# Modulation vectors that are made in later stages, and GpSimd taking one of the two streams throughout

## The chip, the core and the metric

The kernel runs on one core of one Trainium2 chip. The metric is the device time of one execution in microseconds (us). The core has five engines with an instruction queue each: TensorE (PE: matmuls; PEld: its weight loads), VectorE (DVE), ScalarE (ACT), GpSimd (POOL) and SyncE (SP), which here issues all DMA transfers. Each queue is worked off in its written order; an instruction waits until what it needs has been signalled, and everything behind it on that queue waits with it.

## The reference

Two token streams, 256 context tokens and 256 latent tokens of width 1024, go through two layers. Each layer is a feed-forward sub-layer, a token mixer (four branches) and a second feed-forward sub-layer. Every sub-layer is modulated by vectors that a small product makes from a conditioning vector:

```python
act_l = jax.nn.silu(c)
act_c = jax.nn.silu(c_ctx)
for i in range(DEPTH):
    mod_l = (act_l @ w_mod[i] + b_mod[i])[:, None, :]              # nine vectors of 1024
    mod_c = (act_c @ w_mod[i][:, :n_c] + b_mod[i][:n_c])[None, None, :]
    ...
def ffn_sublayer(x, mods, base, g_pre, g_post, w_in, w_out):
    h = modulated_norm(x, g_pre, mods[base], mods[base + 1])       # shift, scale
    return x + 0.5 * mods[base + 2] * rms_norm(swiglu(h, w_in, w_out), g_post)   # gate
```

So a layer has nine modulation vectors for each stream: 0 to 2 (shift, scale, gate) for the first feed-forward sub-layer, 3 to 5 for the mixer, 6 to 8 for the second feed-forward sub-layer. In the last layer the context stream needs only 0 to 4. A vector of both streams takes one 1024 x 1024 block of `w_mod`, 4 MB.

## The kernel before

**Stages.** The program runs through feed-forward stage 1 (layer 0, first), mixer 0, feed-forward stage 2 (layer 0, second), feed-forward stage 3 (layer 1, first), mixer 1 and feed-forward stage 4. Below, "stage" means one of the feed-forward stages. All of them are the function `ffn`, for 512 tokens (the fourth for 256).

**A unit.** In `ffn` a loop runs over 22 slices `f` of the hidden width, called units here. A unit loads two weight tiles of 128 x 1024 (`fin`, 512 KB each), and each is split into a high part and a rest: `wchunk` has ScalarE copy `raw` to `wh` (L220) and VectorE subtract (`wl`, L222). Three matmuls (L228 to L230) for each of eight slices of the width and two weight tiles make the 48 matmuls of a unit. Then ScalarE takes a tanh of the result (L487), VectorE finishes the gated product (L488, L489) and splits it (`gg`). Behind the 22 units stands the output part (`outproj`, 16 weight tiles `foa` and six `fob`, then the norm that begins the next stage).

**The four slots.** Every weight tile and every tile of `w_mod` is loaded into the same rotating buffer, tag `raw`, with four slots (`rp = pool(st, "rp", 4)`). SP's queue issues the loads in order; a load waits there until the last user of its slot is done.

**The modulation vectors.** `mod_steps(l, js, act)` makes vectors `js` of layer `l` in steps. A step loads one 128 x 1024 tile of `w_mod`, eight steps a vector. For the latent stream (`s = 1`) VectorE multiplies the tile by the activation row and sums along it in one instruction (L274, output `jk`). For the context stream (`s = 0`) either GpSimd multiplies in place (L279) and ScalarE sums (L280), or, for layer 0 and `j >= JB = 5`, VectorE does a second product. Where only the latent stream is needed (layer 1, `j >= 5`), even steps go to VectorE and odd ones to GpSimd and ScalarE.

**Who calls the steps.** `stepper(gens, total, skip)` hands out the steps. After each unit `ffn` calls it with weight 2, in the output part with weight `OW = 1` after each of 16 chunks; the first `skip` calls do nothing, and the others add `steps / total` times the weight. The steps start in `st0` (stage 1), `st1` (stage 2) and `st2` (stage 3). PE's order is written out by hand; the other queues are ordered by a scheduler that may move a step ahead by some instructions.

**Who needs the vectors.** `gate_rows(l, base, ...)` in unit 19 of a stage reads vector `base + 2`; `fill0`, `fill1` and `fill2` behind the last unit build the shift and scale of what comes next (`pre_coeff`), used in the norm at the end of the output part. `act_load` loads the two activation rows into the two buffers of `xp`, tag `xr`, which the residual rows `xr` of a stage use too.

Of the kernel before, what the change touches and what calls it, by code (L numbers as in the profile page):

```python
# [79 lines left out]
RAW0 = 16  # L80
WPF = 2
OW = 1.0
JB = 5


def layout(i):
# [77 lines left out]
def build(tc, A):  # L164
# [10 lines left out]
    def dma(o, i):  # L175
        return nc.sync.dma_start(o, i)
# [8 lines left out]
    with st, tc.manual_schedule(engines={mybir.EngineType.PE}):  # L185
# [74 lines left out]
        def mod_steps(l, js, act, raw=None):  # L260
            if callable(act):
                act = act()
            for j in js:
                ss = [1] if l == 1 and j >= 5 else [0, 1]
                for k in range(KT):
                    w = raw() if raw else rp.tile([P, D], F32, tag="raw", name="raw")
                    dma(w, A["wmod"][l, j, k])
                    c = j * KT + k
                    both = l == 0 and j >= JB
                    for s in ss if both else [1]:  # L270
                        if 0 not in ss and k % 2:
                            continue
                        jk = sp.tile([P, D], BF16, tag="sq", name="jk", bufs=1)
                        V.scalar_tensor_tensor(  # L274
                            jk, w, 0.5, act[s], op0=ALU.mult, op1=ALU.mult, accum_out=md[l][:, s, c : c + 1]
                        )
                    if not both and (0 in ss or k % 2):
                        s = ss[0]
                        G.tensor_tensor(w, w, act[s], op=ALU.mult)  # L279
                        S.activation(w, w, AF.Copy, scale=0.5, accum_out=md[l][:, s, c : c + 1])  # L280
                    n = 4 if raw else KT
                    if (k + 1) % n == 0:
                        for s in ss:
                            m = md[l][:, s, c + 1 - n : c + 1]
                            V.tensor_tensor(m, m, bmt[l][:, c + 1 - n : c + 1], op=ALU.add)
                    yield

        def pre_coeff(l, base, gi, streams):
            a = cp.tile([P, 2, KT], F32, tag="pa", name="pa", bufs=2)
            for s in streams:  # L290
                V.scalar_tensor_tensor(
                    a[:, s], md[l][:, s, (base + 1) * KT : (base + 2) * KT], 1.0, ngt[l][:, gi], op0=ALU.add, op1=ALU.mult
                )
                V.tensor_scalar(a[:, s], a[:, s], RMS_D, None, op0=ALU.mult)
            return lambda s, k: (a[:, s, k : k + 1], md[l][:, s, base * KT + k : base * KT + k + 1])

        def gate_rows(l, base, gi, fac, streams):
            gr = cp.tile([P, 2, D], F32, tag="grow", name="grow", bufs=1)
            gc = cp.tile([P, 2, KT], F32, tag="gc", name="gc", bufs=2)
            for s in streams:  # L300
                V.scalar_tensor_tensor(
                    gc[:, s], md[l][:, s, (base + 2) * KT : (base + 3) * KT], fac * RMS_D, ngt[l][:, gi], op0=ALU.mult, op1=ALU.mult
                )
            s0, n = streams[0], len(streams)
            ps = psy.tile([P, 512], F32, tag="py", name="psg")
            T.transpose(ps[: n * KT, :P], gc[:, s0:].rearrange("p s k -> p (s k)"), ident)
            gs = sp.tile([P, 512], F32, tag="t", name="gs")[:, :P]
            S.activation(gs[: n * KT], ps[: n * KT, :P], AF.Copy)
            gd = dp.tile([1, 2 * D], F32, tag="gd", name="gd", bufs=2)
            dma(gd[:, : n * D].rearrange("o (k p) -> (o k) p", p=P), gs[: n * KT])  # L310
            dma(gr[:, s0:].rearrange("p s d -> p (s d)"), gd[:, : n * D].to_broadcast([P, n * D]))
            return gr

        def new_h():
            hh = hp.tile([P, KT, NTOK], F32R, tag="hh", name="hh")
            hl = hp.tile([P, KT, NTOK], F32R, tag="hl", name="hl")
            return hh, hl
# [220 lines left out]
        def act_load():  # L538
            a = [xp.tile([P, D], F32, tag="xr", name="act") for _ in range(2)]
            for s in range(2):  # L540
                dma(a[s], actd[s].to_broadcast([P, D]))
            return a
# [4 lines left out]
        def stepper(gens, total, skip=0):  # L547

            todo = [g for g, _ in gens]
            rate = sum(c for _, c in gens) / total  # L550
            state = {"credit": 0.0, "skip": skip}

            def step(weight):
                if state["skip"]:
                    state["skip"] -= 1
                    return
                state["credit"] += rate * weight
                while todo and state["credit"] > 1e-6:
                    try:
                        next(todo[0])  # L560
                        state["credit"] -= 1.0
                    except StopIteration:
                        todo.pop(0)

            return step
# [15 lines left out]
        with ExitStack() as fs:  # L581
            with ExitStack() as s0:
# [22 lines left out]
                for t in TALL:  # L605
                    xs0[t] = tp.tile([P, D], F32, name=f"x0_{t}")
                raw0 = lambda: tp.tile([P, D], F32, tag="raw0", name="raw0", bufs=RAW0)
                ms0 = mod_steps(0, [0], act, raw0)
                pm = [psy.tile([P, 512], F32, tag="py", name="pm1") for _ in range(2)]

# [95 lines left out]
            def acts0():  # L706
# [2 lines left out]
                        acts.extend(act_load())  # L709
                return acts  # L710

            st0 = stepper([(mod_steps(0, [2, 3, 4], acts0), 24), (mod_steps(0, [5, 6, 7, 8], acts0), 32)], 46, 6)

            def step0(w):
                st0(w)
# [7 lines left out]
        for l in range(L):  # L723
            last = l == L - 1
            toks = TLAT if last else TALL
            streams = [1] if last else [0, 1]

            nx = dict(src=xd, out=None, keep=toks)
            late = mixer(E, l, h, late, toks, streams, nx)
            h = nx["h"]  # L730

            with ExitStack() as fs:
                gp = Gates(fs, f"B{l}")
                if last:
                    n3 = dict(src=xd, out=A["out"], keep=[])
                    ffn(l, 1, h, late, toks, n3, gp, lambda w: None, lambda: gate_rows(l, 6, 5, 0.5, streams), lambda: None)
                else:
                    n3 = dict(src=xd, out=None, keep=TALL)

                    def fill1():  # L740
                        n3.update(coeff=pre_coeff(1, 0, 0, [0, 1]), h=new_h())

                    st1 = stepper([(mod_steps(1, [0, 1, 2, 3, 4], act_load), 40)], 50, 2)
                    late = ffn(l, 1, h, late, toks, n3, gp, st1, lambda: gate_rows(l, 6, 5, 0.5, streams), fill1)
                    h = n3["h"]
            if not last:
                with ExitStack() as fs:
                    gp = Gates(fs, "C")
                    n4 = dict(src=xd, out=None, keep=TLAT)

                    def fill2():
                        n4.update(coeff=pre_coeff(1, 3, 2, [0, 1]), h=new_h())

                    st2 = stepper([(mod_steps(1, [5, 6, 7, 8], act_load), 32)], 50, 2)
                    late = ffn(1, 0, h, late, TALL, n4, gp, st2, lambda: gate_rows(1, 0, 1, 0.5, [0, 1]), fill2)
                    h = n4["h"]

# [1212 lines left out]
```

## Time and profile before

| what | value |
|---|---|
| median of 3 runs | 2695.58 us (2693.67 to 2699.35) |
| the profiled execution | 2695.88 us, its span 2694.1 us |
| TensorE busy, share of the span | 2511.9 us, 93% |
| VectorE | 1765.9 us, 66% |
| ScalarE | 1097.6 us, 41% |
| GpSimd | 711.6 us, 26% |

The span runs from the first to the last instruction of the profiled execution; what the run's own time has beyond it lies before and after. Busy shares are averages over stages with different limits, so the stages are read apart. A busy TensorE is not one at its peak, because matmuls overlap and their ends are modelled: the pace of a stage is read from how long the same count of matmuls takes.

### The profile page before, as it was taken

The numbers are of one execution on the slowest core, as the hardware profiler recorded it, in microseconds if no ns is written. First come the engines' busy times: TensorE is split into PE (matmuls) and PEld (weight loads), VectorE is DVE, ScalarE is ACT, GpSimd is POOL, SyncE is SP. The second block draws the span as 40 slices with busy tenths as digits, with TensorE's granted clock in tenths as the row PEclk, the third lists the DMA queues.
The fourth block names the chain that finished last, engine by engine and source line by source line (L and its number), as shares of the span: only waits on it lengthen the run. The fifth ranks groups of instructions, "written<-read, shape, count | busy, mean of one in ns | idle before, by whom it ended". The sixth has DMA issues, their size and how long they took to land. (4 is left out here: it accounts for less than half of the span.)

```text
span 2694.1 us, 38024 instructions
## 1 busy us (share of the span) xinstructions
PE 2511.9 (93%) x14606; PEld 2113.7 (78%) x14606; DVE 1765.9 (66%) x2547; ACT 1097.6 (41%) x1868; POOL 711.6 (26%) x637
## 2 busy tenths in 40 slices
PE   6978999999999889999999999999999998778998
PEld 3856777887788667888777788888899897677997
DVE  6788885455646898457777555454355678986664
ACT  5435322454543233344343343333255553335443
POOL 4884100100102773002233301111010127860000
PEclk8989999999999999999999999999999998889999
DMA  6345666223232333344445545445423354335564
GB/s 235 106 152 187 212 219 210 83 79 79 79 110 71 85 99 101 94 160 145 164 147 174 179 157 160 160 156 184 137 73 100 108 176 134 114 110 182 162 189 148
DMA packets 134498, 378.55 MB, mean 141 GB/s; under 512 B 26679, under 2 KB 45864, under 8 KB 133548
## 3 DMA queue, kind: packets, MB, share of 16 engines
q1 hardware_dynamic: 134316, 376.11, 43.1%
q8 instruction: 115, 1.88, 0.3%
q14 instruction: 67, 0.55, 0.1%
HBM read 358.14 MB, written 17.91 MB: 140 GB/s over the span
## 5 line engine op out<-in xcount | busy, mean ns | idle before, releaser
L222 DVE TENSOR_TENSOR wl<-raw,wh 128x1024 fp32r<-128x1024 f32 x411 | 567.2, 1380 | 423.9 <-ACT wh L220 417.1
L220 ACT ACTIVATE wh<-raw 128x1024 fp32r<-128x1024 f32 x424 | 447.5, 1056 | 597.0 <-issue 166.0
L230 PE MATMUL pin<-hh,wl 128*128 128x512 f32 (+1 forms) x1468 | 531.5, 362 | 46.5 <-DVE wl L222 46.4
L228 PE MATMUL pin<-hh,wh 128*128 128x512 f32 (+1 forms) x1468 | 530.3, 361 | 8.9 <-DVE hh L356 6.8
L229 PE MATMUL pin<-hl,wh 128*128 128x512 f32 (+1 forms) x1468 | 529.0, 360 | 4.6 <-DVE hl L359 4.3
L279 POOL TENSOR_TENSOR raw<-raw,act 128x1024 f32<-128x1024 f32 x88 | 236.0, 2684 | 480.0 <-DVE jk L274 228.2
L230 PEld LDWEIGHTS pin<-hh,wl 128*128 128x128 f32 x1468 | 282.2, 192 | 96.1 <-DVE wl L222 56.5
L228 PEld LDWEIGHTS pin<-hh,wh 128*128 128x128 f32 x1468 | 282.5, 192 | 52.1 <-DVE hh L356 8.3
L229 PEld LDWEIGHTS pin<-hl,wh 128*128 128x128 f32 x1468 | 281.9, 192 | 47.3 <-DVE hl L359 7.0
L274 DVE SCALAR_TENSOR_TENSOR jk<-raw,act 128x1024 bf16<-128x1024 f32 x152 | 210.8, 1387 | 152.4 <-DMA raw<-wmod 143.2
L249 POOL TENSOR_TENSOR r<-v,mhalf 128x1 f32<-128x1 f32 (+2 forms) x46 | 31.6, 686 | 932.1 <-DVE v L248 833.4
L1090 PE MATMUL pm<-hh,wh 128*128 128x512 f32 (+1 forms) x704 | 254.9, 362 | 0.0
L1091 PE MATMUL pm<-hl,wh 128*128 128x512 f32 (+1 forms) x704 | 247.1, 351 | 0.0
L1092 PE MATMUL pm<-hh,wl 128*128 128x512 f32 (+1 forms) x704 | 246.8, 351 | 0.0
L280 ACT ACTIVATE raw<-raw 128x1024 f32<-128x1024 f32 x88 | 93.2, 1059 | 240.4 <-POOL raw L279 240.4
L403 PE MATMUL y<-wl,gg 128*128 128x512 f32 x448 | 178.2, 398 | 4.0 <-DVE wl L222 3.9
L402 PE MATMUL y<-wh,gg 128*128 128x512 f32 x448 | 177.3, 396 | 0.0
L404 PE MATMUL y<-wh,gg 128*128 128x512 f32 x448 | 177.1, 395 | 0.0
L1090 PEld LDWEIGHTS pm<-hh,wh 128*128 128x128 f32 x704 | 136.7, 194 | 18.3 <-issue 2.5
L1092 PEld LDWEIGHTS pm<-hh,wl 128*128 128x128 f32 x704 | 135.8, 193 | 17.5
L1091 PEld LDWEIGHTS pm<-hl,wh 128*128 128x128 f32 x704 | 136.3, 194 | 15.0
L403 PEld LDWEIGHTS y<-wl,gg 128*128 128x128 f32 x448 | 84.2, 188 | 27.7 <-DVE wl L222 7.9
(425 smaller groups left out, 4829.6 us busy)
## 6 DMA issues: line engine op xcount, KB each, us to landing
raw<-fin SPq DMA_DIRECT2D x176, 512.0 KB, 3.5
raw<-wmod SPq DMA_DIRECT2D x136, 512.0 KB, 4.2
raw<-winf SPq DMA_DIRECT2D x122, 512.0 KB, 3.6
raw<-foa SPq DMA_DIRECT2D x64, 512.0 KB, 3.8
raw<-wbr SPq DMA_DIRECT2D x32, 512.0 KB, 3.6
raw<-fob SPq DMA_DIRECT2D x24, 512.0 KB, 4.1
xd<-xr SPq DMA_DIRECT2D x16, 512.0 KB, 2.9
xr<-xd SPq DMA_DIRECT2D x16, 512.0 KB, 4.9
```

The source lines that it names most:

```text
L220: S.activation(wh, w, AF.Copy)
L222: (G if turns[1] and turns[0] % turns[1] == 0 else V).tensor_tensor(wl, w, wh.bitcast(F32), op=ALU.subtract)
L228: T.matmul(out, lhsT=lh, rhs=rh, start=first and i == 0, stop=False)
L229: T.matmul(out, lhsT=lh, rhs=rl, start=False, stop=False)
L230: T.matmul(out, lhsT=ll, rhs=rh, start=False, stop=last and i == n - 1)
L274: V.scalar_tensor_tensor(jk, w, 0.5, act[s], op0=ALU.mult, op1=ALU.mult, accum_out=md[l][:, s, c : c + 1])
L279: G.tensor_tensor(w, w, act[s], op=ALU.mult)
L402: T.matmul(o, lhsT=lh, rhs=rh, start=kt == 0, stop=False)
L403: T.matmul(o, lhsT=lh, rhs=rl, start=False, stop=False)
L1090: T.matmul(o, lhsT=lh, rhs=rh, start=i == 0, stop=False)
L1091: T.matmul(o, lhsT=lh, rhs=rl, start=False, stop=False)
L1092: T.matmul(o, lhsT=ll, rhs=rh, start=False, stop=i == n - 1)
```

## The change

Three things are edited. `JB` and the second VectorE product go, so that with two streams GpSimd and ScalarE always take the context stream. Vector 8 of layer 0 (8 steps) moves from stage 1 to stage 2. Vectors 2, 3 and 4 of layer 1 (24 steps) move from stage 2 to stage 3, ahead of the 32 steps that were there. The totals that set the rate change with it: 48 steps at 46, skip 6 (were 56); 24 steps at 40, skip 2 (were 40 at 50); 56 steps at 50, skip 2 (were 32). `acts1` and `acts2` load the activation rows once for both lists of a stage.

```diff
-JB = 5
...
                     c = j * KT + k
-                    both = l == 0 and j >= JB
-                    for s in ss if both else [1]:
-                        if 0 not in ss and k % 2:
-                            continue
+                    if 0 in ss or k % 2 == 0:
+                        s = 1
                         jk = sp.tile([P, D], BF16, tag="sq", name="jk", bufs=1)
                         V.scalar_tensor_tensor(
                             jk, w, 0.5, act[s], op0=ALU.mult, op1=ALU.mult, accum_out=md[l][:, s, c : c + 1]
                         )
-                    if not both and (0 in ss or k % 2):
+                    if 0 in ss or k % 2:
                         s = ss[0]
                         G.tensor_tensor(w, w, act[s], op=ALU.mult)
                         S.activation(w, w, AF.Copy, scale=0.5, accum_out=md[l][:, s, c : c + 1])
...
-            st0 = stepper([(mod_steps(0, [2, 3, 4], acts0), 24), (mod_steps(0, [5, 6, 7, 8], acts0), 32)], 46, 6)
+            st0 = stepper([(mod_steps(0, [2, 3, 4], acts0), 24), (mod_steps(0, [5, 6, 7], acts0), 24)], 46, 6)
...
+                    act1 = []
+
+                    def acts1():
+                        if not act1:
+                            act1.extend(act_load())
+                        return act1
...
-                    st1 = stepper([(mod_steps(1, [0, 1, 2, 3, 4], act_load), 40)], 50, 2)
+                    st1 = stepper([(mod_steps(0, [8], acts1), 8), (mod_steps(1, [0, 1], acts1), 16)], 40, 2)
...
-                    st2 = stepper([(mod_steps(1, [5, 6, 7, 8], act_load), 32)], 50, 2)
+                    st2 = stepper([(mod_steps(1, [2, 3, 4], acts2), 24), (mod_steps(1, [5, 6, 7, 8], acts2), 32)], 50, 2)
```

The instructions of TensorE stand in the same order as before. The places below are where the others moved. Lines of the changed kernel are up to three lower in number (L175 for L176, L221 for L222, L271 for L274).

SP's queue near the start of stage 2, before: `wmod` is a tile of a modulation step, `fin` a weight tile, the number is the buffer's name.

```order
L176 DMA raw_10821<-wmod 128x1024
L176 DMA raw_10827<-wmod 128x1024
L176 DMA raw_10833<-fin 128x1024
L176 DMA raw_10864<-fin 128x1024
L176 DMA raw_10902<-wmod 128x1024
L176 DMA raw_10908<-fin 128x1024
L176 DMA raw_10939<-fin 128x1024
```

The same place now:

```order
L175 DMA raw_10771<-wmod 128x1024
L175 DMA raw_10777<-fin 128x1024
L175 DMA raw_10808<-fin 128x1024
L175 DMA raw_10846<-wmod 128x1024
L175 DMA raw_10852<-fin 128x1024
L175 DMA raw_10883<-fin 128x1024
```

Units with two steps and with one took turns; now a unit has one step, and every fifth has two.

SP's queue near the start of stage 3, before:

```order
L176 DMA raw_13583<-wmod 128x1024
L176 DMA raw_13587<-fin 128x1024
L176 DMA raw_13618<-fin 128x1024
L176 DMA raw_13656<-wmod 128x1024
L176 DMA raw_13660<-fin 128x1024
L176 DMA raw_13691<-fin 128x1024
L176 DMA raw_13729<-wmod 128x1024
L176 DMA raw_13733<-wmod 128x1024
```

The same place now:

```order
L175 DMA raw_13605<-wmod 128x1024
L175 DMA raw_13613<-wmod 128x1024
L175 DMA raw_13619<-fin 128x1024
L175 DMA raw_13650<-fin 128x1024
L175 DMA raw_13688<-wmod 128x1024
L175 DMA raw_13694<-wmod 128x1024
L175 DMA raw_13700<-wmod 128x1024
L175 DMA raw_13706<-fin 128x1024
L175 DMA raw_13737<-fin 128x1024
```

Steps of one stream, one or two a unit, have become steps of two streams, two or three a unit, until the 24 of them are done; the steps of one stream follow at the same rate.

VectorE's queue in the output part of stage 1, before: `jk` is a product of a step (`act_1304` the context row, `act_1305` the latent row), `wl` the split of a weight tile.

```order
L274 SCALAR_TENSOR_TENSOR jk_2953,md0_95<-raw_2949,act_1305 128x1024
L222 TENSOR_TENSOR wl_2922<-raw_2919,wh_2921 128x1024
L274 SCALAR_TENSOR_TENSOR jk_2987,md0_95<-raw_2985,act_1304 128x1024
L274 SCALAR_TENSOR_TENSOR jk_2989,md0_95<-raw_2985,act_1305 128x1024
L274 SCALAR_TENSOR_TENSOR jk_2993,md0_95<-raw_2991,act_1304 128x1024
L222 TENSOR_TENSOR wl_2958<-raw_2955,wh_2957 128x1024
```

The same place now:

```order
L221 TENSOR_TENSOR wl_2920<-raw_2917,wh_2919 128x1024
L271 SCALAR_TENSOR_TENSOR jk_3023,md0_95<-raw_3021,act_1305 128x1024
L221 TENSOR_TENSOR wl_2956<-raw_2953,wh_2955 128x1024
L271 SCALAR_TENSOR_TENSOR jk_3059,md0_95<-raw_3057,act_1305 128x1024
L221 TENSOR_TENSOR wl_2994<-raw_2991,wh_2993 128x1024
```

Between two splits two to four products of VectorE have become one; the context products of these steps stand on GpSimd now.

## Rows read from the trace of the kernel before

**Rows 1.** Windows of stage 1 (three), stage 2 (two), stage 3 (two): start:end, length, busy

```profile
core 0: us, PE busy (x) PEld busy (x) DVE busy (x) ACT busy (x) POOL busy (x), PEclk, DMA share, GB/s
110.00:260.00 150.00, 122.89 (x494) 96.86 (x493) 120.64 (x161) 64.47 (x97) 108.05 (x96) 0.91 0.47 158
260.00:364.00 104.00, 95.69 (x414) 76.52 (x413) 90.41 (x138) 34.29 (x51) 13.86 (x4) 1.00 0.63 208
364.00:494.00 130.00, 125.91 (x546) 100.15 (x544) 86.45 (x138) 40.17 (x65) 3.45 (x7) 1.00 0.57 188
1216.40:1483.50 267.10, 250.78 (x1147) 206.60 (x1146) 199.56 (x208) 108.16 (x168) 85.30 (x36) 0.98 0.46 159
1483.50:1608.20 124.70, 124.69 (x545) 100.53 (x544) 62.37 (x82) 48.16 (x79) 25.32 (x13) 1.00 0.50 166
1608.00:1853.10 245.10, 243.09 (x1147) 203.98 (x1146) 128.75 (x162) 90.46 (x133) 38.64 (x16) 1.00 0.51 163
1853.10:1977.20 124.10, 124.10 (x545) 100.71 (x544) 50.36 (x68) 41.51 (x67) 8.11 (x8) 1.00 0.40 132
```

**Rows 2.** Matmuls of the projections: ns min/median/max, first and last start; stages 2, 3

```profile
L228 PE MATMUL pin<-hh,wh x376: 278/389/632, 1216.4 to 1482.7; 128*128 128x512 f32 x164, 128*128 128x256 f32 x24
...
L228 PE MATMUL pin<-hh,wh x376: 278/389/478, 1608.0 to 1852.3; 128*128 128x512 f32 x164, 128*128 128x256 f32 x24
```

**Rows 3.** Timeline of ScalarE, the tanh of a unit: start, length; stages 2, 3

```profile
1341.10 0.58 ACT L487 ACTIVATE t<-pin 128x512 f32<-128x512 f32 x1
...
1352.07 0.57 ACT L487 ACTIVATE t<-pin 128x512 f32<-128x512 f32 x1
...
1364.80 0.57 ACT L487 ACTIVATE t<-pin 128x512 f32<-128x512 f32 x1
...
1378.18 0.58 ACT L487 ACTIVATE t<-pin 128x512 f32<-128x512 f32 x1
...
1674.27 0.58 ACT L487 ACTIVATE t<-pin 128x512 f32<-128x512 f32 x1
...
1685.11 0.58 ACT L487 ACTIVATE t<-pin 128x512 f32<-128x512 f32 x1
```

**Rows 4.** Timeline of VectorE over one unit of stage 2 with two steps

```profile
1355.38 1.22 DVE L274 SCALAR_TENSOR_TENSOR jk<-raw,act 128x1024 bf16<-128x1024 f32 x1 [1.96 <-DMA raw<-wmod]
...
1357.13 3.10 DVE L274 SCALAR_TENSOR_TENSOR jk<-raw,act 128x1024 bf16<-128x1024 f32 x1
...
1360.76 3.08 DVE L222 TENSOR_TENSOR wl<-raw,wh 128x1024 fp32r<-128x1024 f32 x1
...
1364.93 1.23 DVE L222 TENSOR_TENSOR wl<-raw,wh 128x1024 fp32r<-128x1024 f32 x1 [0.48 <-ACT wh L220]
```

**Rows 5.** Timelines of SP, GpSimd and ScalarE over the same unit

```profile
1351.24 2.54 SPq L176 DMA_DIRECT2D raw<-wmod  x2
1360.36 3.84 SPq L176 DMA_DIRECT2D raw<-fin  x2
...
1356.74 2.41 POOL L279 TENSOR_TENSOR raw<-raw,act 128x1024 f32<-128x1024 f32 x1 [8.05 <-DMA raw<-wmod]
1360.37 2.39 POOL L279 TENSOR_TENSOR raw<-raw,act 128x1024 f32<-128x1024 f32 x1 [1.22 <-ACT raw L280]
...
1362.80 1.06 ACT L280 ACTIVATE raw<-raw 128x1024 f32<-128x1024 f32 x1 [1.29 <-POOL raw L279]
```

**Rows 6.** TensorE's waits from 50 to 364 us, and from 1217 to 1483 us

```profile
PE pin L230 <- DVE wl L222: 33.1, 13, 8.5
...
PE pin L230 <- DVE wl L222: 13.2, 9, 2.4
```

**Rows 7.** Windows of the split's line alone, VectorE: late stage 1, and stage 2

```profile
260.00:364.00 104.00, 19.45 (x16) 0.00 (x0) 1.00 0.63 208
1217.00:1483.00 266.00, 86.30 (x42) 0.00 (x0) 0.98 0.46 158
```

**Rows 8.** The page's groups: the latent product of all steps

```profile
L274 DVE SCALAR_TENSOR_TENSOR jk<-raw,act 128x1024 bf16<-128x1024 f32 x152 | 210.8, 1387 | 152.4 <-DMA raw<-wmod 143.2
```

More of the change, by code (lines that the diff above doesn't have):

```diff
@@ L749, in build, with acts2 @@
                     n4 = dict(src=xd, out=None, keep=TLAT)
+                    act2 = []
+                    def acts2():
+                        if not act2:
+                            act2.extend(act_load())
+                        return act2
                     def fill2():
                         n4.update(coeff=pre_coeff(1, 3, 2, [0, 1]), h=new_h())
-                    st2 = stepper([(mod_steps(1, [5, 6, 7, 8], act_load), 32)], 50, 2)
+                    st2 = stepper([(mod_steps(1, [2, 3, 4], acts2), 24), (mod_steps(1, [5, 6, 7, 8], acts2), 32)], 50, 2)
                     late = ffn(1, 0, h, late, TALL, n4, gp, st2, lambda: gate_rows(1, 0, 1, 0.5, [0, 1]), fill2)
```

## The prediction

> **What bounds the kernel now.** I read the seven stretches first [rows 1]. TensorE is what the span is made of: in the projection part of the second and of the third feed-forward stage it issues the same 1147 matmuls, yet the first of the two takes 267.1 us and the other 245.1 us. The matmuls there run from 1216.4 and from 1608.0 us [rows 2]. The 22.0 us between them are the whole price of the modulation work in stage 2, since the output parts that follow are alike (124.7 and 124.1 us). Stage 3 has TensorE busy from end to end at a granted clock of 1.00; stage 2 has 0.98.
>
> Next, the pace of a unit (two weight tiles, 48 matmuls). From one ScalarE tanh to the next a unit of stage 3 takes 10.84 us; in stage 2 a unit with one modulation step takes 10.97 us, and the two after it, with two steps each, 12.73 and 13.38 us [rows 3]. The reader is to see why in VectorE's and the other queues' rows [rows 4, 5]: all loads turn in four `raw` slots. Two `wmod` tiles are asked for at 1351.24 to 1353.8 us. GpSimd multiplies them one after the other from 1356.74 and 1360.37 us, 3.63 us apart; only when ScalarE has summed each may a weight tile be asked for, at 1360.36 us and after 1363.8 us. Meanwhile VectorE's split `wl` that TensorE waits for stands behind both of VectorE's products and itself takes 3.08 us instead of 1.22 us. So the loop of slots lasts 13.4 us where TensorE needs 10.84 us. The waits say the same: TensorE stands 13.2 us for `wl` in stage 2, 33.1 us in stage 1 [rows 6].
>
> Third, the splits: 16 of them take 19.45 us (1.22 us each) where GpSimd is mostly idle, 42 take 86.30 us (2.05 us each) in stage 2, where GpSimd multiplies [rows 7]. So a product given to GpSimd is not free for VectorE: 42 x 0.83 = 35 us over the 34 products there (the 36 operations of rows 1 less two powers), about 1.0 us each, against the mean 1.39 us of a product that VectorE does itself [rows 8].
>
> The Trainium skill (SBUF — State Buffer, section Who interferes with whom) has a rule that speaks against the change: a VectorE instruction with two SBUF inputs and a GpSimd one that reads SBUF exclude each other, and the later one waits the other out. The stretched splits agree with it. By it the 24 products handed over in stage 1 relieve VectorE of nearly nothing, stage 1's second stretch below would cost 13 us instead of 7, and the forecast would be 2711 us.
>
> **The change part by part.** The order of TensorE's own instructions is the same. A step below is one 512 KB tile of `wmod`; a two-stream step is one VectorE product, one GpSimd product and one ScalarE sum.
>
> Stage 2. Of 40 two-stream steps 32 stood in the 20 units that take steps (1.6 a unit, twelve units with two); now 24 stand there (1.2 a unit, four units with two) and none beside the output part, where their removal is worth nothing because TensorE is busy for 124.69 of its 124.7 us. The 22.0 us come to 1.83 us for each second step. Left are 4 x 1.83 = 7.3 us: **14.7 us less**. Bounds: if lone double units catch up wholly, 22.0 less; if the price goes with all steps, 22.0 x 8/32 = 5.5 less. I take the second-step price, because the single unit of rows 3 keeps nearly the pace of stage 3. The eighth vector is ready long before its gate row is wanted, and the first layer-1 coefficients, now finished with the last unit, stand on VectorE ahead of the output part and are first used at its end: nothing.
>
> Stage 3. It had 32 one-stream steps and no loss. It gets 24 two-stream steps in front of them, at 2.24 a unit: by the queue's order about eight units with two and two units with three, ten in all, without single ones between. The nearest row is the second of two double units, 13.38 us, 2.54 us over 10.84; a third step adds GpSimd's pitch of 3.63 us. That makes 10 x 2.54 + 2 x 3.63 = 32.7 us. By the mean price of stage 2, 14 second and third steps x 1.83 = 25.6 us. The first double unit eats a lead and not TensorE's time, so I take **29 us more**, between them; the lower bound, all steps alike, is 24 x 22.0/32 = 16.5 us, the upper 37 us, if the triple units also break the prefetch of the next. Behind them the 32 one-stream steps are run at 2.24 a unit instead of 1.28. Each holds its slot for VectorE or for GpSimd, not for both, and stage 3 shows no idle time with some units of two such steps: **1 us more**, between 0 and 8. One `xr` load now waits in SP's queue for GpSimd's last context product, with the next four loads behind it; once, and under 5 us, within that bound.
>
> Stage 1. 56 steps become 48: eight fewer loads, VectorE products 88 to 48, GpSimd products and ScalarE sums 24 to 48, 2.43 steps a unit to 2.09. Three stretches at 10.84/48 = 0.226 us a matmul [rows 1, 3]. From 110 to 260 us 494 matmuls need 111.6 us of the 150, 38.4 us are lost, also to the state-space set-up on GpSimd and VectorE. About ten units there lose 0.34 step each, mostly a third one; at 2.54 to 3.63 us that is 9 to 12 us: **10 less** (0 to 19, half the loss). From 260 to 364 us, where both streams were on VectorE, 414 matmuls need 93.6 us and 10.4 us are lost; with GpSimd's loop in its place 8.6 units with 1.09 second steps at 1.83 us lose 17 us: **7 more** (5 less if VectorE's relief counts, 13 more at the 2.54 us of steady double units). The output part took 130.0 us for 546 matmuls, 5.6 us over its twins; VectorE's bursts of two to four products between splits become one: **3 less** (6 less to 4 more, as GpSimd then holds slots there too). Together 6 less.
>
> Loads as such cost nothing: the 16 DMA engines are half busy in all these stretches [rows 1]. Nor does ScalarE, under half busy.
>
> Sum: -14.7 + 29 + 1 - 6 = +9.3 us. The profiled execution took 2695.88 us, 1.8 us outside its span of 2694.1 us, and lies 0.3 us above the median 2695.58 us of the runs. 2695.88 + 9.3 = **2705.2 us**.
>
> **The rivals.**
> VectorE's relief decides (faster). Stage 1 loses 40 of 88 VectorE products, at 1.39 us some 56 us of an engine that is busy for 120.64 of 150 and 90.41 of 104 us there. If its loss of 38.4 + 10.4 + 5.6 = 54.4 us goes with these products, 54.4 x 40/88 = 24.7 us vanish; with stage 3 at 25.6 us: -24.7 - 14.7 + 25.6 + 1 = -12.8, 2683 us. For it speaks that VectorE is the engine named in the waits; against it, that GpSimd's products stretch the splits, and that the dearest stretch (110 to 260 us) had GpSimd's form already. It decides as soon as stage 1 gains over 16 us.
>
> The steps only change places (no change). Lone double units in stage 2 cost nothing (22.0 us less), stage 3 takes 25.6 us, the rest 6 us less: -2.4, 2693.5 us. For it: TensorE's lead at the start of a stretch; against it: nothing but the rhythm of twelve double units has been seen.
>
> GpSimd's loop is the bound wherever it stands (much slower). Steady units of two and three in stage 3 cost the full 32.7 us and the steps behind them 5, stage 1's second stretch 13 and its output part 4, first stretch 10 less, stage 2 14.7 less: +30, 2726 us. By the Trainium skill's rule (SBUF — State Buffer, Who interferes with whom) it would come out on this side.
>
> **How the numbers follow.** My sum gets 0.40, the relief 0.23, no change 0.22, the full loop 0.15. The likeliest one's own range is 2697 to 2714 us. The range of 8 in 10 reaches from the relief's time to just short of the full loop's: 2682 to 2724 us. A measurement of this kernel can tell about 0.2%, 5.4 us, from no change: below 2690.2 faster, above 2701.0 slower. Slower holds 0.36 of my sum, all of the full loop and 0.03 of no change, 0.54; faster 0.20 of the relief and 0.04 of no change, 0.24; the same 0.22.
>
> **What would show it.** Stage 2's projections at about 252 us for 1147 matmuls; stage 3's at about 275 us, with units of 13 to 16 us up to the middle and 10.9 us after it, TensorE waiting for `wl`, and splits near 2 us; stage 1 from 110 us to its end a few us shorter, with splits of 2 us and GpSimd busy in the 104 us where it now has 13.86. I am wrong if stage 3 keeps under 262 us, or if stage 1 loses more than 16 us.

## The result, and the profile after

The changed kernel takes 2723.01 us (median of 4 runs, 2719.47 to 2731.76) against 2695.76 us: ratio 1.0104, interval 1.0086 to 1.0122, slower by 1.0%. Its profiled execution took 2722.43 us with a span of 2720.6 us, 26.5 us more than before. The forecast was 2705.2 us, its range ended at 2724: the direction is right, the size is short by 18 us.

The windows of the changed kernel, cut at the same places of the program as [rows 1] (stage 1 in three, stages 2 and 3 in two):

```profile
core 0: us, PE busy (x) PEld busy (x) DVE busy (x) ACT busy (x) POOL busy (x), PEclk, DMA share, GB/s
110.00:260.00 150.00, 126.15 (x509) 98.49 (x508) 118.05 (x157) 63.09 (x94) 101.17 (x95) 0.92 0.45 152
260.00:371.10 111.10, 96.77 (x395) 76.30 (x394) 82.66 (x94) 46.18 (x72) 44.55 (x16) 0.95 0.52 176
371.10:506.00 134.90, 129.16 (x546) 101.00 (x544) 70.19 (x99) 55.02 (x93) 44.59 (x19) 0.99 0.53 172
1230.00:1488.70 258.70, 248.72 (x1147) 205.39 (x1146) 156.01 (x188) 99.08 (x152) 68.02 (x26) 0.99 0.46 154
1488.70:1612.80 124.10, 124.10 (x546) 100.87 (x544) 45.49 (x61) 39.41 (x63) 3.30 (x6) 1.00 0.36 121
1612.80:1876.30 263.50, 249.75 (x1147) 206.67 (x1145) 188.26 (x212) 109.80 (x172) 100.51 (x38) 0.98 0.55 186
1876.30:2004.10 127.80, 125.27 (x546) 100.52 (x544) 54.53 (x78) 45.83 (x75) 14.11 (x11) 1.00 0.46 156
```

Against [rows 1] the same 1147 matmuls of stage 2 take 258.7 us instead of 267.1, those of stage 3 263.5 instead of 245.1; stage 1's output part takes 134.9 instead of 130.0, and GpSimd, busy there for 3.45 us before, is busy for 44.59 us. In the table below the parts are cut at the first `pin` and `y` matmul of each stage (so they may differ from a window by a few tenths); the column "ahead" is the time before stage 1's first `pin` matmul. Mixer 0 is 1.4 us longer, mixer 1 0.9 shorter, stage 4 0.6 longer.

| us | ahead | stage 1 projections | its output part | stage 2 | its output | stage 3 | its output |
|---|---|---|---|---|---|---|---|
| before | 51.3 | 312.4 | 130.0 | 267.0 | 124.7 | 244.9 | 124.3 |
| after | 50.9 | 320.2 | 134.9 | 258.7 | 124.1 | 263.5 | 127.8 |
| difference | -0.4 | +7.8 | +4.9 | -8.3 | -0.6 | +18.6 | +3.5 |

The pace of a unit, ScalarE's tanh in the changed kernel (start, length), four of stage 2 and four of stage 3:

```profile
1346.97 0.58 ACT L484 ACTIVATE t<-pin 128x512 f32<-128x512 f32 x1
...
1358.45 0.58 ACT L484 ACTIVATE t<-pin 128x512 f32<-128x512 f32 x1
...
1374.11 0.58 ACT L484 ACTIVATE t<-pin 128x512 f32<-128x512 f32 x1
...
1383.99 0.58 ACT L484 ACTIVATE t<-pin 128x512 f32<-128x512 f32 x1
...
1735.92 0.58 ACT L484 ACTIVATE t<-pin 128x512 f32<-128x512 f32 x1
...
1750.29 0.58 ACT L484 ACTIVATE t<-pin 128x512 f32<-128x512 f32 x1
...
1762.10 0.57 ACT L484 ACTIVATE t<-pin 128x512 f32<-128x512 f32 x1
...
1779.23 0.58 ACT L484 ACTIVATE t<-pin 128x512 f32<-128x512 f32 x1
```

In stage 2 a single unit takes 11.48 us, the double unit after it 15.66 us and the next 9.88 us; before, a single unit took 10.97 and the second of two double ones 13.38 us [rows 3]. In stage 3 they go up and down: 14.37, 11.81, 17.13 us. Standing alone is not what makes that double unit dear, because the kernel before has lone ones too: the one that ends with the first tanh of [rows 3] took 13.49 us. The tanh at its start and the loads of its two steps, before:

```profile
1327.61 0.57 ACT L487 ACTIVATE t<-pin 128x512 f32<-128x512 f32 x1
...
1327.05 2.26 SPq L176 DMA_DIRECT2D raw<-wmod  x2
```

There the second tile is asked for 1.9 us after the first (2.26 less the 0.33 us of an issue); in the unit below it is 6.6 us, and the three double units of the changed stage 2 take 15.44 to 15.99 us.

The queues over that double unit of stage 2, in the changed kernel: SP's, VectorE's, GpSimd's and ScalarE's timeline (in brackets the idle time before an instruction and what ended it):

```profile
1358.37 6.92 SPq L175 DMA_DIRECT2D raw<-wmod  x2
...
1362.56 1.22 DVE L271 SCALAR_TENSOR_TENSOR jk<-raw,act 128x1024 bf16<-128x1024 f32 x1 [3.62 <-DMA raw<-wmod]
...
1363.71 1.22 DVE L221 TENSOR_TENSOR wl<-raw,wh 128x1024 fp32r<-128x1024 f32 x1
...
1370.09 3.06 DVE L221 TENSOR_TENSOR wl<-raw,wh 128x1024 fp32r<-128x1024 f32 x1
...
1363.92 3.27 POOL L276 TENSOR_TENSOR raw<-raw,act 128x1024 f32<-128x1024 f32 x1 [8.97 <-DVE jk L271]
1369.71 2.37 POOL L276 TENSOR_TENSOR raw<-raw,act 128x1024 f32<-128x1024 f32 x1 [2.51 <-DVE jk L271]
...
1367.23 1.06 ACT L277 ACTIVATE raw<-raw 128x1024 f32<-128x1024 f32 x1 [8.20 <-POOL raw L276]
...
1368.29 1.05 ACT L219 ACTIVATE wh<-raw 128x1024 fp32r<-128x1024 f32 x1
```

Read it as a chain: the step's tile is asked for at 1358.37 and used at 1362.56; the second step's tile is asked for 6.6 us later, at about 1364.95, as the split that began at 1363.71 behind that product ends; GpSimd begins only after VectorE's product of the same tile and takes 3.27 us; ScalarE has stood idle for 8.20 us in front of the sum, and the weight copy `wh`, next in its queue, runs at 1368.29 (by the order in which slots come free, its tile is the `fin` asked for at 1352.70, so it was there long before); the split of that weight begins at 1370.09 and, beside GpSimd's second product, lasts 3.06 us. The prediction had seen the slots wait [rows 4, 5]; it had not seen that the sum stands in ScalarE's queue ahead of the copy.

TensorE's waits in the changed kernel, from 50 to 371 us, in stage 1's output part, and in stages 2 and 3 (us in total, times, longest):

```profile
PE pin L229 <- DVE wl L221: 32.7, 15, 6.6
...
PE y L400 <- DVE wl L221: 4.2, 7, 1.6
...
PE pin L229 <- DVE wl L221: 7.2, 5, 2.5
...
PE pin L229 <- DVE wl L221: 10.6, 6, 3.0
```

Against [rows 6] stage 1's projections wait as long as before (33.1 us) although the stage as a whole has eight steps and 40 of VectorE's products fewer, and they are 7.8 us longer all the same; stage 2's waits fall from 13.2 us, stage 3's are new.

### The profile page after: what moved, and what is told of

Same layout as the page of the kernel before. It is cut to its first block, busy times and chain, and to the rows that moved or that the text cites. A ratio compares the mean times of both kernels' runs of the same rounds, so it can differ in the third digit from the quotient of the medians.

```text
span 2720.6 us, 38093 instructions
## 1 busy us (share of the span) xinstructions
PE 2526.2 (93%) x14606; PEld 2116.9 (78%) x14606; DVE 1740.7 (64%) x2483; ACT 1129.0 (41%) x1932; POOL 808.2 (30%) x669
## 5 line engine op out<-in xcount | busy, mean ns | idle before, releaser
L221 DVE TENSOR_TENSOR wl<-raw,wh 128x1024 fp32r<-128x1024 f32 x411 | 567.7, 1382 | 429.6 <-ACT wh L219 422.9
L276 POOL TENSOR_TENSOR raw<-raw,act 128x1024 f32<-128x1024 f32 x120 | 332.5, 2772 | 527.2 <-DVE jk L271 381.4
L271 DVE SCALAR_TENSOR_TENSOR jk<-raw,act 128x1024 bf16<-128x1024 f32 x120 | 174.2, 1451 | 200.6 <-DMA raw<-wmod 190.6
L277 ACT ACTIVATE raw<-raw 128x1024 f32<-128x1024 f32 x120 | 127.1, 1059 | 402.4 <-POOL raw L276 402.4
```

What stands on the lines that cost most here:

```text
L221: (G if turns[1] and turns[0] % turns[1] == 0 else V).tensor_tensor(wl, w, wh.bitcast(F32), op=ALU.subtract)
```

## The experiments

Two theories. A: what is dear is GpSimd's product and the sum behind it, because both in-order queues (ScalarE's copies, VectorE's splits) stand behind them. B: what is dear is the number of loads that turn in four slots, whoever multiplies. Ratios are against the kernel before. Diffs are against it too, unless said otherwise. Stage times are read from one profiled execution each, which lay between 4 us below and 8 us above the median of its kernel, so differences of a few us between two runs' stages prove little.

**1. GpSimd's edit alone.**

```diff
-                    both = l == 0 and j >= JB
+                    both = False
```

> The kernel before with the one edit that GpSimd and ScalarE take the context stream of all two-stream steps; no vector moves, so stage 1 still has 56 steps. Theory A (GpSimd's product in place of VectorE's second one is what stage 1 lost by): from 260 us to the end of stage 1 it loses at least the 15 us that the full change lost there (10.5 in the projections, 4.9 in the output part), more with 56 steps than with 48: 2711 to 2722 us, stages 2 and 3 unchanged at 391.8 and 369.2 us. Theory B (stage 1 lost by the order that the lower rate gave it, and VectorE's relief helps): within 5 us of 2695.

Measured: 2709.41 us, ratio 1.0061 (1.0045 to 1.0078); stage 1's parts 319.9 and 135.9 us, stages 2 and 3 as before (266.7, 245.6). So this edit alone, with 56 steps instead of 48, makes a loss in stage 1 like the change's, +7.5 and +5.9 us: half of the change's 27 us. The time lies just under theory A's range.

**2. The moves alone** (the three lists as in the change, `JB` kept).

> All moves of the change, but layer 0's vectors 5 to 7 keep both streams on VectorE. Theory A: stage 1 does not lose the 12 us but gains a few by 8 fewer steps, stage 2 gains its 9 us, stage 3 with its output part loses its 22 us: about 2704 us, 2698 to 2710. Theory B: stage 1 loses here too, 2715 us or more.

Measured: 2711.71 us, ratio 1.0072 (1.0052 to 1.0091). Stage 1 310.6 and 138.3 us, stage 2 254.0, stage 3 261.5 and 131.2. Between the two expectations: the output part of stage 1 lost 8.3 us with fewer steps, which neither foresaw (runs 8 and 9). Runs 1 and 2 lose 15 and 17 us, the change with both edits 27: the two do not simply add.

**3. Layer 1's vectors 2 to 4 moved, nothing else.**

```diff
-                    st1 = stepper([(mod_steps(1, [0, 1, 2, 3, 4], act_load), 40)], 50, 2)
+                    st1 = stepper([(mod_steps(1, [0, 1], act_load), 16)], 40, 2)
...
-                    st2 = stepper([(mod_steps(1, [5, 6, 7, 8], act_load), 32)], 50, 2)
+                    st2 = stepper([(mod_steps(1, [2, 3, 4], acts2), 24), (mod_steps(1, [5, 6, 7, 8], acts2), 32)], 50, 2)
```

> Only vectors 2 to 4 of layer 1 move from stage 2 to stage 3; vector 8 of layer 0 stays in stage 1, and layer 0 keeps both streams on VectorE for vectors 5 to 8. Stage 1 as before. If a second step of a unit is what costs, stage 2 with 16 steps in 20 units loses nothing: 22 us less, and stage 3 with its output part 22 us more: 2695 us, 2690 to 2701. If single units cost too, as the 11.5 us units of the changed kernel suggest (0.65 us each), stage 2 gains only 10 to 14 us: 2703 to 2708 us.

Measured: 2696.85 us, ratio 1.0007 (0.9995 to 1.0019). Stage 2 gains 21.2 us (245.8: with 16 steps, 0.8 a unit, GpSimd's products cost 0.9 us over stage 3's 244.9), stage 3 loses 19.3 and 4.3. The move by itself is a change of places.

**4. The changed kernel with stage 3's two-stream steps wholly on VectorE.**

```diff
+                    if l == 1 and j in (2, 3, 4):
+                        jk = sp.tile([P, D], BF16, tag="sq", name="jk", bufs=1)
+                        V.scalar_tensor_tensor(
+                            jk, w, 0.5, act[0], op0=ALU.mult, op1=ALU.mult, accum_out=md[l][:, 0, c : c + 1]
+                        )
-                    if 0 in ss or k % 2:
+                    elif 0 in ss or k % 2:
```

> The changed kernel, but the 24 two-stream steps of stage 3 have both products on VectorE, with as many loads and the same rate. Theory A (the loop through GpSimd and ScalarE holds the slots and ScalarE's queue): stage 3's units with two steps come near 12 us and splits to 1.22 us, its projections lose 5 to 12 us instead of 18.5: 2708 to 2717 us. Theory C (more loads than slots is what costs, on whatever engine): no change, 2719 to 2726 us.

Measured: 2712.42 us, ratio 1.0069 (1.0049 to 1.009); stage 3 252.6 and 129.6 us. The loads are the same and the slots as many, and 10.9 of the 18.6 us are gone, as A said. The other 7.7 us stay, so A is not all; and without GpSimd and the sum each slot is also held for a shorter time, so the hold is not ruled out (run 7).

**5. The kernel before with stage 2's two-stream steps on VectorE** (`both = 0 in ss and (l == 1 or j >= JB)`).

> The kernel before, with the 40 two-stream steps of stage 2 (layer 1, vectors 0 to 4) put wholly on VectorE; nothing is moved. If GpSimd's product and the sum that follows it in ScalarE's queue are what makes a double unit dear (theory A: a double unit with both products on VectorE ran at 10.8 to 11.2 us where vector 8 was moved into stage 2), stage 2's projections fall from 267 us to 246 to 254 us, stages 1 and 3 stay within 3 us, and the time is 2675 to 2685 us, ratio 0.992 to 0.996. If the loads and the occupied slots are what costs (theory B), or if two products per step overload VectorE (40 more, at 1.39 us 55 us of an engine that has to split 44 tiles there as well), stage 2 stays at 262 us or more and the time at 2690 us or more.

Measured: 2689.37 us, ratio 0.9983 (0.9972 to 0.9993). Stage 2 258.7 us, 8.3 less, its output part 128.5, 3.8 more: A's expectation missed, between both. Double units, after the first two, still took 13.3 to 14.9 us. The same kind of unit in this kernel (SP's, VectorE's and ScalarE's timeline):

```profile
1375.58 7.15 SPq L176 DMA_DIRECT2D raw<-wmod  x2
...
1379.87 1.23 DVE L274 SCALAR_TENSOR_TENSOR jk<-raw,act 128x1024 bf16<-128x1024 f32 x1 [3.72 <-DMA raw<-wmod]
...
1382.29 1.22 DVE L222 TENSOR_TENSOR wl<-raw,wh 128x1024 fp32r<-128x1024 f32 x1
...
1374.99 1.05 ACT L220 ACTIVATE wh<-raw 128x1024 fp32r<-128x1024 f32 x1
```

ScalarE no longer waits: the copy is done at 1376.04. But VectorE stands idle for 3.72 us in front of a product whose tile was only asked for at 1375.58, and the split behind its two products, which could have run since 1376.04, begins at 1382.29. So a second cost exists that B names in part: a step asked for late blocks VectorE's queue while its tile is on the way.

**6. Every two-stream step on VectorE** (`both = 0 in ss`; nothing moved).

> The kernel before, with every two-stream step put wholly on VectorE (layer 0, vectors 2 to 8, and layer 1, vectors 0 to 4); GpSimd keeps only half of the one-stream steps. Theory A (GpSimd's product and the sum behind it are the cost): stage 2 gains as in the run above, 13 to 21 us, and stage 1's stretch from 110 to 260 us, which has 24 such products on GpSimd, gains a further 3 to 12 us: 2665 to 2680 us. Rival (VectorE is the bound of that stretch, where it is busy for 120.64 of 150 us): 24 more products of 1.39 us there cost 10 to 33 us, and the time is 2685 to 2715 us, with stage 1's projections at 322 to 345 us instead of 312.

Measured: 2655.28 us, ratio 0.9859 (0.9843 to 0.9876): faster than both kernels and than expected. Windows of this kernel, cut like stage 1's three in [rows 1] (the first two begin 8 us earlier, as the stage does, and the third where the output part begins):

```profile
102.00:252.00 150.00, 133.00 (x553) 106.91 (x552) 128.54 (x237) 52.04 (x67) 55.21 (x78) 0.93 0.58 183
252.00:332.60 80.60, 80.60 (x356) 66.46 (x355) 73.59 (x121) 24.24 (x33) 0.00 (x0) 1.00 0.72 237
332.60:457.00 124.40, 124.39 (x546) 100.88 (x544) 81.16 (x131) 39.82 (x64) 3.35 (x7) 1.00 0.57 188
```

and TensorE's wait for the split from 43 to 332 us:

```profile
PE pin L230 <- DVE wl L222: 14.6, 2, 9.9
```

The first stretch holds 553 matmuls where it held 494 [rows 1]: 59 x 0.226 = 13 us, from taking some 20 products off GpSimd and giving them to VectorE, which was already 80% busy there. VectorE is busier (128.54 us), and TensorE waits 18.5 us less for it. Ahead of stage 1 another 8.1 us go, with the eight steps made there. In the second stretch nothing is lost any more: its 356 matmuls need 80.5 of the 80.6 us, where 10.4 us were lost before. So VectorE's time was not what bound stage 1. GpSimd was busy for 108.05 of the 150 us of the first stretch [rows 1] and is busy for 55.21 now; how much of the gain is its own backlog there, how much the stretched splits and how much ScalarE's queue is not separated.

**7. The changed kernel, slots freed ahead of the sum** (stage 3: GpSimd writes its product into a tile of its own).

```diff
-                        G.tensor_tensor(w, w, act[s], op=ALU.mult)
-                        S.activation(w, w, AF.Copy, scale=0.5, accum_out=md[l][:, s, c : c + 1])
+                        g = q() if q else w
+                        G.tensor_tensor(g, w, act[s], op=ALU.mult)
+                        S.activation(g, g, AF.Copy, scale=0.5, accum_out=md[l][:, s, c : c + 1])
```

> The changed kernel, with GpSimd writing its product of stage 3's steps into a tile of its own (one, in bf16) instead of over the loaded tile, so that the slot is free as soon as both products are made and not only when ScalarE has summed. If the hold of the four slots by the sum is the cost of stage 3's double and triple units, its projections fall from 263.5 us to 248 to 256 us and the time to 2707 to 2716 us. If the cost is that the sum stands ahead of the weight copy in ScalarE's in-order queue and waits there for GpSimd, or that GpSimd's products stretch VectorE's splits, they stay at 260 to 266 us and the time within 3 us of 2722 us.

Measured: 2741.0 us, ratio 1.0171 (1.0154 to 1.0188); stage 3 283.5 and 133.0 us. Neither: by the medians 18 us worse than the changed kernel. Waits in stage 3's projections, first two of the changed kernel, then three of this one, and GpSimd's group from 1609 to 1890 us in this one:

```profile
DVE jk L271 <- DMA raw<-wmod: 38.5, 14, 7.2
...
POOL raw L276 <- ACT raw L277: 9.8, 8, 1.2
...
DVE jk L271 <- DMA raw<-wmod: 76.2, 27, 8.2
...
POOL q L277 <- ACT q L278: 12.6, 10, 1.3
...
PE pin L229 <- DVE wl L221: 21.8, 12, 4.0
...
L277 POOL TENSOR_TENSOR q<-raw,act 128x1024 bf16<-128x1024 f32 x35 | 100.3, 2866 | 173.3 <-DMA raw<-wmod 148.2 <-ACT q L278 12.6 <-ACT gg L232 6.8
```

The one tile ties each product to the sum before it, but that wait is hardly new: 12.6 us, against 9.8 us in the changed kernel. What doubled is VectorE's idle time in front of steps whose tile was still on the way, 76.2 us instead of 38.5, and TensorE's wait for the split with it, 21.8 us instead of 10.6: the cost that run 5 showed. Freeing the slot early did not help, but since the loads came later for a reason that was not found, the hold of the slots by the sum is not separated from the order of ScalarE's queue.

**8 and 9. The pace in stage 1.** Run 2, and then the changed kernel, with stage 1's 48 steps at the old rate, so that they end sooner (`..., 46, 6)` becomes `..., 39.4, 6)`).

> The moves alone (both products of layer 0's vectors 5 to 7 on VectorE, as before), with stage 1's 48 remaining steps paced as before the change (1.22 a weight tile) so that they end sooner, instead of stretched over the same units. With the stretched pace the moves alone gave stage 1 310.6 + 138.3 us, against 312.4 + 130.0 us before. If steps beside the output part are what costs there, the output part falls to 124 to 129 us, the projections stay at 310 to 315 us, and the time is 2701 to 2706 us. If the cost of a step is the same wherever it stands, the sum of both parts stays at 446 to 451 us and the time at 2709 to 2714 us.

> The changed kernel with stage 1's 48 steps at the pace of before (1.22 a weight tile), so that they end sooner; GpSimd keeps one stream throughout. If the loss beside stage 1's output part comes from the even alternation of one step and one weight tile there (theory: the loop of four slots then takes 6.1 us a weight tile where TensorE needs 5.4), the output part falls from 134.9 to 124 to 127 us, the projections stay within 3 us of 320.2 us, and the time is 2711 to 2717 us. If it comes from GpSimd's products, which are still made there and in the units ahead of it, the output part stays at 131 us or more, or the projections take what it gives back, and the time is 2719 us or more.

Measured, moves alone: 2700.99 us, ratio 1.002 (1.001 to 1.003), stage 1 313.4 and 124.3 us: as the first theory said, 14 us less in the output part than in run 2. Measured, changed kernel: 2723.29 us, ratio 1.0095 (1.0078 to 1.0111), stage 1 319.3 and 131.8 us: the rival. With the products on VectorE the pace decides in the output part; with GpSimd in the loop it gives 3 us, and the whole gains nothing. The other runs agree: at 1.22 steps a weight tile and with vectors 5 to 8 on VectorE the output part took 124.3 to 130.0 us (the kernel before, runs 3, 5, 6, 8, 11 and 12), at 1.04 it took 136.5 and 138.3 (runs 10 and 2).

**10. The change's moves with every two-stream step on VectorE.**

> The changed kernel's moves (layer 0's vector 8 to stage 2, layer 1's vectors 2 to 4 to stage 3) with every two-stream step on VectorE instead of one stream on GpSimd throughout. If GpSimd's products are what made the change slow, all of stage 1's loss goes: stage 1 takes 280 to 290 + 124 us (372 us more of span than that is not left: 320.2 + 134.9 in the changed kernel), stage 2 251 to 256 us, stage 3 252 to 255 + 130 us, together 2650 to 2660 us, some 65 us under the changed kernel. If the moves themselves carry the loss, it stays at 2690 us or more.

Measured: 2668.26 us, ratio 0.9906 (0.9891 to 0.9922), 55 us under the changed kernel. This run differs from it only in who makes the context product. Stage 2: 245.3 us instead of 258.7, so GpSimd's form is the whole of what was left there. Stage 1: 290.8 instead of 320.2 us. Stage 3: 258.1 instead of 263.5. The gain is 10 us short of the expected 65, so the time misses its range. Stage 2 beat its range (251 to 256), stage 1's projections ended just above theirs, and two parts were clearly dearer: stage 3 (252 to 255), and stage 1's output part, 136.5 us where run 6, with 13 steps in it, took 124.3. There, VectorE's timeline in this kernel:

```profile
360.82 1.23 DVE L274 SCALAR_TENSOR_TENSOR jk<-raw,act 128x1024 bf16<-128x1024 f32 x1 [3.64 <-DMA raw<-wmod]
...
361.98 1.22 DVE L222 TENSOR_TENSOR wl<-raw,wh 128x1024 fp32r<-128x1024 f32 x1
...
366.72 1.23 DVE L274 SCALAR_TENSOR_TENSOR jk<-raw,act 128x1024 bf16<-128x1024 f32 x1 [2.18 <-DMA raw<-wmod]
...
367.87 1.22 DVE L222 TENSOR_TENSOR wl<-raw,wh 128x1024 fp32r<-128x1024 f32 x1
```

At 1.04 steps a weight tile step and tile alternate strictly: in these lines each split stands behind a product that waited for its tile, and the second split comes 5.9 us after the first, where TensorE's 24 matmuls a tile want 5.4. It looks like run 5's blocking; why run 6's equally many steps there stay free is not shown.

**11 and 12. Fewer moved.** Every two-stream step on VectorE, layer 0's vector 8 left in stage 1, and of layer 1 either vectors 2 to 4 or only 3 and 4 moved to stage 3.

> Every two-stream step on VectorE, and layer 1's vectors 2 to 4 moved to stage 3 (layer 0's vector 8 stays in stage 1). If the price of a move is set by how closely the steps stand and by who makes the products, both terms add: stage 2 gives back 18 us against the run with every step on VectorE (259.3 + 128.9 to 246 + 124), stage 3 takes 11 us (247.2 + 124.3 to 252.6 + 129.6, as where the changed kernel's stage 3 ran on VectorE), sum -7, 2645 to 2652 us. If moving steps into stage 3 costs the same whoever makes the products (22 us or more), it is 2655 to 2662 us.

> As the run before this one, with only layer 1's vectors 3 and 4 moved (24 two-stream steps in stage 2 over 21 units, 16 of them and the 32 one-stream steps in stage 3). If what costs is a unit with two or more steps, stage 2 has 3 or 4 such units and takes 247 to 252 us, stage 3 takes 247 to 252 us with its output part at 124 to 128 us: 2640 to 2650 us, at or a little under the run with vectors 2 to 4 moved. If each step costs the same wherever it stands (no gain from spreading), 2651 to 2658 us.

Measured: 2658.03 us, ratio 0.987 (0.9852 to 0.9887), and 2640.86 us, ratio 0.9805 (0.9789 to 0.982). The first misses: stage 2 is free (245.2) but stage 3 takes 257.6 and 130.5 us. Its time lies in the range of the rival, which wanted 22 us more or above in stage 3 and its output part; against run 6 they are 17 us longer. The second meets its expectation, with stage 2 better than expected, and is the best kernel here, 82 us under the changed one. Its windows of stages 2 and 3 (projections):

```profile
1179.90:1425.20 245.30, 242.84 (x1147) 203.85 (x1146) 154.76 (x224) 74.18 (x105) 2.03 (x2) 1.00 0.47 152
1549.30:1797.50 248.20, 244.28 (x1147) 205.20 (x1146) 160.82 (x232) 89.44 (x129) 36.07 (x15) 0.99 0.58 190
```

24 two-stream steps in stage 2 cost 0.4 us over stage 3's undisturbed 244.9 (0.96 a unit here, 1.2 in run 10); 40 of them (1.6 a unit, runs 5 and 6) cost 13.8 and 14.4. In stage 3, 16 of them ahead of the 32 others (1.92 steps a unit, of both kinds) cost 3.3 us, 24 (2.24 a unit) 7.7 to 13.2 in runs 4, 10 and 11. So with VectorE making both products a stage has room for about one two-stream step a unit at no cost, and beyond that the price rises faster than the number of steps; these few points do not show where the rise begins.

## Why the prediction was right in direction and short in size

The sum gave 9.3 us more, the span grew by 26.5. By parts the miss is +18.7 us in stage 1, +6.4 in stage 2, -7.9 in stage 3 and next to nothing elsewhere. The errors of stages 2 and 3 nearly cancel, which is luck, and the measured time lies inside the range by one us.

**Stage 1 is the step that failed.** The sum said 6 us less (-10, +7, -3); its projections and output part measured 12.7 us more.
- First stretch, 110 to 260 us: 509 matmuls instead of 494, 15 x 0.226 = 3.4 us less, not 10. The term priced third steps; what cost time there were GpSimd's products (20 of them begin in that stretch before, 19 after), which the change left in place. Run 6 takes them away and gains 13 us in that stretch.
- Second stretch: 395 matmuls need 89.3 of 111.1 us, 21.8 lost against 10.4: 11.4 us more, not 7. The mechanism (GpSimd's loop in place of VectorE's products) is borne out by run 1; the mean price of 1.83 us a second step was too low, and the 13 us kept as a bound were nearer. The waits named do not hold all of it: the granted clock of this stretch fell from 1.00 to 0.95, in short spells at 1.2 instead of 2.4 GHz around TensorE's longest waits (0.92 from 278 to 300 us, 0.87 from 318 to 345 us). That is at most 0.05 x 111.1 = 5.6 us of the 11.4, an estimate from these rows.
- Output part: 4.9 us more, not 3 less; just past its upper bound of 4. VectorE's burst of products between splits was no cost: with one product and GpSimd in its place the output part got longer (run 1, by 5.9 us), and the slower pace of the steps costs there too (runs 8 and 9).

**Stage 2**: -14.7 forecast, -8.3 measured, between the bounds -22 and -5.5. The mechanism was right, the size wrong: the price of a second step, 1.83 us, was a mean of the old rhythm, and in the new one a double unit took 15.44 to 15.99 us, at least 4.6 us above 10.84, of which the next unit gives back about 1. Its second tile is asked for later than in the old rhythm (6.6 us after the first, not 1.9); that this is the reason is not shown. Runs 3 and 10 show that the cost lies in what GpSimd adds: 16 of its steps, one a unit, are free, 24 cost 13 us, 24 on VectorE nothing.

**Stage 3**: +30 forecast, +18.6 and +3.5 = 22 measured, between 16.5 and 37, and 263.5 us lies just above the 262 us under which it would have been refuted. Units of 11 to 17 us up to the middle, shorter ones of 9.5 to 13.6 us behind them but for the last, the wait for `wl`, and splits of 1.56 us (42 in 65.64 us, about 2 were forecast) are there. The sum was too high because the first four units behind the stage's opening took only 10.85 to 12.07 us and a unit after a long one catches up (11.81 after 14.37 us). Of the loss, 5 to 11 us are GpSimd's form (runs 10 and 4, whose equal steps differ by 5.5 us in stage 3); the rest stays with VectorE making both products, so it comes with how closely the steps stand.

**The rivals.** The relief of VectorE is refuted, and more: VectorE got work back in run 6 and the kernel became faster. No change fails by stage 1, and by the double units of stage 2, which were not free (8.3 us gained, not 22.0). The full loop gave 2726 us and came nearest, with stage 1's second stretch and output part as it had them, but its stage 3 was too dear by 16 us, its first stretch and its stage 2 too cheap by 7 and 6: that it came so near is in part luck. On the rule of the Trainium skill (SBUF — State Buffer, section Who interferes with whom), the trace agrees that both sides stretch: GpSimd's product from 2.37 to 3.27 us (begun at 1363.92, beside the split that ended at 1364.93), the split from 1.22 to 3.06 us (begun at 1370.09, beside the product that ended at 1372.08). In both pairs the later one is longer by about what the earlier one still had to run. The forecast of 2711 us that the prediction drew from it was still too low: it had the second stretch about right (13 us, measured 11.4) and left the first stretch, the output part and stage 2 as they were, which came out 6.6, 7.9 and 6.4 us dearer.

## What to carry to other kernels

Before an engine is given work because another is named in the waits, look at what stands behind the new result in every in-order queue: here the handed-over product had cost 1.4 us on VectorE and now put a sum ahead of ScalarE's weight copies. Price a step by the unit it falls in and by its rhythm, not by a mean: with both products on VectorE 24 steps in stage 2 were free and 40 cost 14 us. A busy engine that waits behind a slower one looks like a shortage; giving it the whole work is the test.

## What the runs showed that was not expected

Work taken off GpSimd (busy for 108.05 of 150 us) and put on VectorE, which was busier still (120.64 of 150 us), made that stretch faster: 553 matmuls instead of 494 in 150 us. And two kernels with the same steps in stage 3 (runs 4 and 10) took 252.6 and 258.1 us for it. Whether that is how the stage is entered or scatter between executions is not shown; either way terms of that size are not read from one stage of one run.
